# RWKV state of two heads as one block-diagonal 128x128 tile with full products, in a decoder-layer kernel

## The chip, the cores and the metric

The kernel runs on one core of one Trainium2 chip. The metric is the time of one execution on the device in microseconds (us); lower is better. The times of several executions are given as their median with the lowest and the highest. One further execution was taken with the hardware profiler, and all rows shown here come from it.

## The reference

One decoder layer on 2048 tokens of width 1024, in float32. Eight RWKV-7 heads and eight dilated-attention heads of 64 channels each work side by side; then follow an output projection, a layer norm, a mixture of 32 experts with a gated embedding, and a second layer norm. The change concerns the recurrence of the RWKV heads alone:

```python
def step(state, inp):
    r_t, w_t, k_t, v_t, a_t, b_t = inp
    sa = jnp.einsum('bhvk,bhk->bhv', state, a_t)
    state = (state * w_t[:, :, None, :] + sa[..., None] * b_t[:, :, None, :]
             + v_t[..., None] * k_t[:, :, None, :])
    y_t = jnp.einsum('bhvk,bhk->bhv', state, r_t)
    return state, y_t
...
_, y = lax.scan(step, state0, xs)
```

Each head has a state of 64x64, which each token decays, corrects and adds to, and which each token reads.

## The kernel before, in words

`run` (L1945) goes through stages: `project` (input projections and, at its end, `rwkv_prep`, which prepares the RWKV operands and the decays), `mixers` (the recurrence and the attention), `mix_out`, `route`, `ple`, `experts` and `finish`. The change lies in `mixers`.

The recurrence is done in chunks of 128 tokens. Eight heads make four units `u` of two heads, one head in partitions 0 to 63 and the other in 64 to 127 (`H[0]`, `H[1]`). The 2048 tokens make eight column blocks `q` of two chunks `c` each, so there are 4 x 8 x 2 = 64 chunks. A round is a pair of units at one `q`; there are 16 rounds. For each round, `rwkv_front` and `rwkv_inverse` invert the triangular matrices of the chunks, and `rwkv_state` (two streams, `i` = 0 for units 0 and 2, `i` = 1 for units 1 and 3) does the rest. In it:

- L814 to L818 make the masked score matrices: `RB`, and `MJ`, a tile of 2x2x192 elements a partition (head, chunk, 128 score columns and 64 columns of keys). L831 copies the transposed keys into columns 128 to 191 of both (ScalarE); L828 copies the transposed values, `vt`.
- L840 multiplies by `WF`, the inverse's result, and L843 (VectorE, 128x384, once per head) adds the product to all 192 columns of `MJ`.
- L848 makes `pq`; L851 (VectorE) adds the identity to its last 64 columns, giving `E`, 64 columns per chunk with the two heads in the two partition halves, and L854 adds to the rest, giving `Q`.
- Then, for each chunk, in order: L862 (ScalarE) scales the old state by the decay `rho`, giving `st`. L867 and L869 are the new state, for each head the keys of `MJ` times `vt`, plus `E` times `st`, each with 64 columns; L872 (ScalarE) copies it out as `raw`. L877 and L879 are the output, for each head `vt` times the scores of `MJ`, plus `st` times `Q`, 128 columns each, into the head's half of the output partitions; L881 copies it out. L869 and L879 contract over 64 partitions, L867 and L877 over 128; each writes 64 output partitions.

```python
mm(pn[H[h]], MJ[:, h, c, P:192], vt[:, c, H[h]], start=True, stop=first)
if not first:
    mm(pn[H[h]], E[H[h], c], st[H[h]], start=False, stop=True)
...
mm(py[H[h]], vt[:, c, H[h]], MJ[:, h, c, 0:P], start=True, stop=first)
if not first:
    mm(py[H[h]], st[H[h]], Q[H[h], c], start=False, stop=True)
```

The first chunk of all has no old state, and the last computes no new one. Each stream has two PSUM buffers (`self.rps[i]`) for everything it computes, used in turn.

The order of the work: `mixers` hands its streams (two of states, two of inverses, two of fronts, one that combines attention passes, three of attention blocks) to `weave`. A stream yields what its next piece will cost on which engine (`_pe(300)` is 300 ns of TensorE, `_act`, `_dve` and `_pool` give the cost of so many elements), and `weave` lets the stream go on that could start first, attention first while it lags behind a set pace (`late`). The framework's scheduler then puts the instructions of each engine in their final order, with this order as its input; in this stage TensorE's order is not fixed by hand. Other lines of the stage that the text names: L734 (128x128 products with 128 columns, of the inverse), L814 (products of 64 partitions), L717 and L1080 (transposes of 128x128), L1055 and L1058 (attention scores), L1094 (attention output, 64 output partitions per head, the heads one after the other), L1071 (attention's row minimum on VectorE), L665 (GpSimd copies of a front), L676 (a GpSimd memset).

SBUF pools: the recurrence's pools lie on the right side, `rf` among them, and are opened in `rwkv_setup` when the projection's pools close; a tile waits for the tiles that lay in its memory before.

Of the kernel before, what the change touches and what calls it, by code (L numbers as in the profile page):

```python
# [9 lines left out]
F32 = mybir.dt.float32  # L10
F32R = mybir.dt.float32r
I32 = mybir.dt.int32
AF = mybir.ActivationFunctionType
ALU = mybir.AluOpType
# [4 lines left out]
P = 128  # L19
S = 2048  # L20
# [98 lines left out]
def _act(n):  # L119
    return "ACT", 190 + 0.56 * n  # L120


def _dve(n):
    return "DVE", 60 + 1.06 * n
# [6 lines left out]
def _pe(ns):  # L131
    return "PE", ns
# [35 lines left out]
class K:  # L168
# [344 lines left out]
    def rwkv_setup(self, es):  # L513
        tc = self.tc

        pool = lambda name, bufs=1, **k: es.enter_context(tc.tile_pool(name=name, bufs=bufs, reuse_waits="tile", **k))
        self.rl = pool("rl", 2 * ROUNDS, side="right")
        self.rf = pool("rf", side="right")
        self.rv_ = pool("rvt", 2 * ROUNDS, side="right")
        self.rk_ = pool("rk", side="right")  # L520
        self.rps = [pool(f"rps{n}", 2, space=PSUM) for n in range(2)]
        self.state = [None] * 4

        self.small = [self.rf.tile([P, 16, 16], F32, name=name) for name in ("A64", "V64", "tm")]

# [269 lines left out]
    def rwkv_state(self, i, u, q, pp):  # L795

        nc, kp = self.nc, self.rk_
        mm = nc.tensor.matmul
        ps = lambda: self.rps[i].tile([P, BT], F32, name=f"ps{i}", tag=f"ps{i}")
        T = lambda name, shape, bufs=1: kp.tile(shape, F32, name=f"{name}{i}", tag=f"{name}{i}", bufs=bufs)  # L800
        RB = T("RB", [P, 2, 2, 192])
        H = [slice(0, 64), slice(64, 128)]
        col = [slice(c * P, (c + 1) * P) for c in range(2)]
        while "v" not in pp:
            yield None
        rt, v = ([pp[m][:, cs] for cs in col] for m in ("rt", "v"))
        bk = [pp["bk"][:, c] for c in range(2)]
        MJ = T("MJ", [P, 2, 2, 192])
        for h in range(2):
            yield _pe(900)  # L810
            pr = ps().rearrange("p (c k s) -> p c k s", c=2, k=2)
            for c in range(2):
                for m in range(2):
                    mm(pr[:, c, m], bk[c][H[h], m], rt[c][H[h]], start=True, stop=True)  # L814
            yield _dve(2 * P)
            nc.vector.tensor_tensor(out=RB[:, h, :, 0:P], in0=pr[:, :, 0, :], in1=self.c("upi").unsqueeze(1).to_broadcast([P, 2, P]), op=ALU.mult)
            yield _dve(2 * P)
            nc.vector.tensor_tensor(out=MJ[:, h, :, 0:P], in0=pr[:, :, 1, :], in1=self.c("upi").unsqueeze(1).to_broadcast([P, 2, P]), op=ALU.mult)  # L818
        vt = T("vt", [P, 2, P])
        for m in range(2):  # L820
            yield _pe(430 - 215 * m)
            pt = ps().rearrange("p (k s) -> p k s", s=P)
            for j in range(2 - m):
                for c in range(2):
                    nc.tensor.transpose(pt[:, 2 * j + c], v[c] if m else bk[c][:, j], self.c("eye"))
            yield _act((4 - 2 * m) * P)
            if m:
                nc.scalar.copy(vt, pt[:, 0:2])  # L828
            else:
                for j in range(2):  # L830
                    nc.scalar.copy((RB, MJ)[j][:, :, :, P:192], pt[:, 2 * j:2 * j + 2].rearrange("p c (h k) -> p h c k", h=2))  # L831
        while "WF" not in pp:
            yield None
        WF = pp["WF"]
        pm = []
        for h in range(2):
            yield _pe(660)
            pm.append(ps()[:, 0:384].rearrange("p (c s) -> p c s", s=192))
            for c in range(2):
                mm(pm[h][:, c], WF[:, h, c, 64:192], RB[:, h, c], start=True, stop=True)  # L840
        for h in range(2):
            yield _dve(384)
            nc.vector.tensor_tensor(out=MJ[:, h], in0=pm[h], in1=MJ[:, h], op=ALU.add)  # L843
        yield _pe(700)
        pq = ps()[:, 0:384].rearrange("p (c s) -> p c s", s=192)
        for c in range(2):
            for h in range(2):
                mm(pq[H[h], c], WF[:, h, c, 0:64], RB[:, h, c], start=True, stop=True)  # L848
        yield _dve(128)
        E = T("E", [P, 2, 64])  # L850
        nc.vector.tensor_tensor(out=E, in0=pq[:, :, P:192], in1=self.c("eye2").unsqueeze(1).to_broadcast([P, 2, 64]), op=ALU.add)  # L851
        yield _dve(256)
        Q = T("Q", [P, 2, P])
        nc.vector.tensor_tensor(out=Q, in0=pq[:, :, 0:P], in1=pp["rt"].rearrange("p (c s) -> p c s", s=P), op=ALU.add)  # L854
        yt = T("yt", [P, 2 * P])
        for c in range(2):
            first = q == 0 and c == 0
            last = q == 7 and c == 1
            if not first:
                yield _act(64)  # L860
                st = T("st", [P, 64], 2)
                nc.scalar.activation(st, self.state[u], AF.Copy, scale=pp["rho"][:, c:c + 1])  # L862
            if not last:
                yield _pe(300)
                pn = ps()[:, 0:64]
                for h in range(2):
                    mm(pn[H[h]], MJ[:, h, c, P:192], vt[:, c, H[h]], start=True, stop=first)  # L867
                    if not first:
                        mm(pn[H[h]], E[H[h], c], st[H[h]], start=False, stop=True)  # L869
                yield _act(64)  # L870
                raw = T("raw", [P, 64], 4)
                nc.scalar.copy(raw, pn)  # L872
                self.state[u] = raw
            yield _pe(600)
            py = ps()[:, 0:P]
            for h in range(2):
                mm(py[H[h]], vt[:, c, H[h]], MJ[:, h, c, 0:P], start=True, stop=first)  # L877
                if not first:
                    mm(py[H[h]], st[H[h]], Q[H[h], c], start=False, stop=True)  # L879
            yield _act(128)  # L880
            nc.scalar.copy(yt[:, col[c]], py)  # L881
        nc.sync.dma_start(self.y[u * P:(u + 1) * P, q * 2 * P:(q + 1) * 2 * P], yt)
        pp["done"] = True
# [1098 lines left out]
```

## Time and profile before

| | us |
|---|---|
| median of 3 executions (lowest to highest) | 3423.52 (3413.01 to 3430.57) |
| the profiled execution | 3428.44 |
| its span, first to last instruction | 3426.5 |
| busy in the span: TensorE matmuls | 3088.4 |
| TensorE weight loads | 2425.0 |
| VectorE | 2084.3 |
| ScalarE | 1546.0 |
| GpSimd | 666.5 |

PE is TensorE's matmuls, PEld its weight loads, DVE is VectorE, ACT ScalarE, POOL GpSimd, SP the engine that issues most DMAs. A line such as L877 is that line of the kernel. PEclk, the granted clock, is the mean share of 2.4 GHz that TensorE's clock had; it has two levels, 1.2 and 2.4 GHz. Matmuls are pipelined and their ends are modelled: a matmul's duration says less than the distance from its start to the next one's start. An fp32 matmul leaves two records. A few per cent of the matmul records can be missing.

### The profile page before, as it was taken

The numbers are of one execution on the slowest core, as the hardware profiler recorded it, in microseconds if no ns is written. First come the engines' busy times: TensorE is split into PE (matmuls) and PEld (weight loads), VectorE is DVE, ScalarE is ACT, GpSimd is POOL, SyncE is SP. The second block draws the span as 40 slices with busy tenths as digits, with TensorE's granted clock in tenths as the row PEclk, the third lists the DMA queues.
The fourth block names the chain that finished last, engine by engine and source line by source line (L and its number), as shares of the span: only waits on it lengthen the run. The fifth ranks groups of instructions, "written<-read, shape, count | busy, mean of one in ns | idle before, by whom it ended". The sixth has DMA issues, their size and how long they took to land. (4 is left out here: it accounts for less than half of the span.)

```text
span 3426.5 us, 49694 instructions
## 1 busy us (share of the span) xinstructions
PE 3088.4 (90%) x17038; PEld 2425.0 (71%) x17039; DVE 2084.3 (61%) x4542; ACT 1546.0 (45%) x3710; POOL 666.5 (19%) x663
## 2 busy tenths in 40 slices
PE   8989759998899998998999789999999999998880
PEld 6667648776676776777778567778878777786560
DVE  4996324685653643554644768773377778775756
ACT  3443112564444533444434333331177777675642
POOL 0441000353100200200200212222111111111215
PEclk9999879999897977799878799999999999999895
DMA  5213341788525324315310545323289999997745
GB/s 164 80 56 111 81 77 70 218 271 263 114 54 110 86 69 93 84 43 115 101 35 12 143 143 172 112 104 131 80 291 311 321 312 321 308 294 256 277 144 199
DMA packets 364111, 533.21 MB, mean 156 GB/s; under 512 B 92376, under 2 KB 204736, under 8 KB 363840
## 3 DMA queue, kind: packets, MB, share of 16 engines
q1 hardware_dynamic: 333240, 463.94, 43.3%
q0 software_dynamic: 14208, 45.74, 5.7%
q10 hardware_dynamic: 16408, 20.33, 1.8%
q8 instruction: 136, 2.23, 0.3%
q14 instruction: 119, 0.97, 0.1%
HBM read 402.40 MB, written 128.06 MB: 155 GB/s over the span
## 5 line engine op out<-in xcount | busy, mean ns | idle before, releaser
L1697 DVE TENSOR_TENSOR wl<-raw,wh 128x512 fp32r<-128x512 f32 x768 | 477.9, 680 | 89.5 <-ACT wh L1696 89.2
L1696 ACT CAST wh<-raw 128x512 fp32r<-128x512 f32 x768 | 417.3, 620 | 9.8 <-DMA raw<-in_w_up_dram 9.4
L198 PE MATMUL ps<-xh,wh 128*128 128x512 f32 x640 | 263.3, 411 | 0.4 <-ACT xh L322 0.4
L199 PE MATMUL ps<-xl,wh 128*128 128x512 f32 x640 | 259.5, 405 | 1.0 <-DVE xl L323 1.0
L200 PE MATMUL ps<-xh,wl 128*128 128x512 f32 x640 | 258.5, 404 | 0.0
L1074 ACT ACTIVATE pe<-pe,ms 128x256 f32<-128x256 f32 (+1 forms) x384 | 175.3, 458 | 120.1 <-DVE ms L1071 116.0
L1826 POOL DMA_INDIRECT acc<-ysb,ix x48 | 95.8, 1995 | 624.9 <-ACT ysb L1825 401.6
L198 PE MATMUL pe<-wh,XX 128*128 128x512 f32 x480 | 199.2, 415 | 3.8 <-ACT wh L1696 3.8
L199 PE MATMUL pe<-wl,XX 128*128 128x512 f32 x480 | 191.6, 399 | 2.6 <-DVE wl L1697 2.6
L200 PE MATMUL pe<-wh,XX 128*128 128x512 f32 x480 | 190.2, 396 | 0.0
L198 PEld LDWEIGHTS ps<-xh,wh 128*128 128x128 f32 x640 | 125.3, 196 | 34.5 <-issue 2.8
L1071 DVE CUSTOM_DVE_ANT_0 pe<-pl,bias 128x256 f32<-128x256 f32 x216 | 83.5, 420 | 104.3 <-PE pl L1055 75.9
L199 PEld LDWEIGHTS ps<-xl,wh 128*128 128x128 f32 x640 | 125.0, 195 | 30.2 <-DVE xl L323 2.5
L200 PEld LDWEIGHTS ps<-xh,wl 128*128 128x128 f32 x640 | 124.5, 194 | 29.6
L1080 PE MATMUL pl<-eye,pe 128*128 128x128 f32 x600 | 135.1, 318 | 7.7 <-ACT pe L1074 6.1
L1055 PE MATMUL pl<-KK,Q 128*128 128x256 f32 x432 | 118.8, 405 | 16.1 <-DMA KK<-ks 14.9
L1094 PE MATMUL po<-pe,V 128*64 128x128 f32 x1200 | 131.5, 326 | 1.8 <-DVE O L1106 1.3
L198 PE MATMUL pb<-gh,XH 128*128 128x512 f32 x320 | 126.1, 394 | 0.0
L199 PE MATMUL pb<-gl,XH 128*128 128x512 f32 x320 | 125.4, 392 | 0.0
L200 PE MATMUL pb<-gh,XL 128*128 128x512 f32 x320 | 124.9, 390 | 0.0
L1741 PE MATMUL pe<-wh,XX 128*128 128x512 f32 x288 | 119.5, 415 | 5.4 <-ACT wh L1696 5.4
L1742 PE MATMUL pe<-wl,XX 128*128 128x512 f32 x288 | 118.1, 410 | 2.9 <-DVE wl L1697 2.9
(412 smaller groups left out, 7799.8 us busy)
## 6 DMA issues: line engine op xcount, KB each, us to landing
raw<-in_w_gate_dram SPq DMA_DIRECT2D x128, 512.0 KB
raw<-in_w_up_dram SPq DMA_DIRECT2D x128, 512.0 KB
raw<-in_w_down_dram SPq DMA_DIRECT2D x128, 512.0 KB
pk<-pk SPq DMA_DIRECT2D x32, 512.0 KB
pk_t<-pk SPq DMA_DIRECT2D x32, 512.0 KB
KK<-ks SPq DMA_DIRECT2D x64, 256.0 KB
wr<-in_w_in_dram SPq DMA_DIRECT2D x48, 256.0 KB
rkk<-rkk SPq DMA_DIRECT2D x32, 384.0 KB
```

Of the source, the lines that this page charges most:

```text
L198: mm(out, lh, rh, start=first, stop=False)
L199: mm(out, lh, rl, start=False, stop=False)
L200: mm(out, ll, rh, start=False, stop=last)
L1055: mm(pl[:, h], q, toks(KK[:, m, h], n, prev, 2), start=m == 0, stop=m == 1)
L1074: nc.scalar.activation(pe[:, h, w], pe[:, h, w], AF.Exp, bias=m_[h], scale=-1.0, accum_out=s_[h])
L1080: nc.tensor.transpose(pt[:, h, b], pe[:, h, b * P:(b + 1) * P], self.c("eye"))
L1094: mm(o[h * 64:(h + 1) * 64, j], vb[:, h * 64:(h + 1) * 64], tt[:, h, b], start=b == kb[0], stop=b == 1)
L1696: nc.scalar.copy(wh[:, c], raw[:, c])
L1697: nc.vector.tensor_tensor(out=wl[:, c], in0=raw[:, c], in1=wh.bitcast(F32)[:, c], op=ALU.subtract)
L1741: mm(ps, L[:, 0:P], wh, start=first, stop=False)
L1742: mm(ps, L[:, 0:P], wl, start=False, stop=last)
L1826: nc.gpsimd.indirect_dma_start(out=self.acc, out_offset=bass.IndirectOffsetOnAxis(ap=ix[0:r, e, b:b + 1], axis=0), in_=ysb[0:r], in_offset ...
```

## The change

The state of a unit's two heads becomes one 128x128 tile with a head's 64x64 state in each diagonal block, zero elsewhere. Each unit has two such tiles, used in turn; they and two tiles `E`, block-diagonal too, are allocated and cleared once by GpSimd. The new state is one full product of the keys (a tile `MK` of its own) with `vt` plus one of `E` with the state; only the diagonal blocks are copied out, one by ScalarE and one by VectorE, already scaled by the next chunk's `rho`, so the separate scaling is gone. The output takes the two per-head products with the scores as before and one full product of the state with `Q`. The add into `MJ` is split in two, one for the scores and one for the keys, and `E` is written by two instructions. The costs that `rwkv_state` yields to `weave` change with it.

```diff
-        self.state = [None] * 4
+        self.state = [[self.rf.tile([P, P], F32, name=f"S{u}{n}") for n in range(2)] for u in range(4)]
+        self.E = [self.rf.tile([P, 2, P], F32, name=f"E{i}") for i in range(2)]
+        for t in (*(t for ts in self.state for t in ts), *self.E):
+            self.nc.gpsimd.memset(t, 0.0)
...
-        MJ = T("MJ", [P, 2, 2, 192])
+        MJ, MK = T("MJ", [P, 2, 2, P]), T("MK", [P, 2, P])
...
-                for j in range(2):
-                    nc.scalar.copy((RB, MJ)[j][:, :, :, P:192], pt[:, 2 * j:2 * j + 2].rearrange("p c (h k) -> p h c k", h=2))
+                nc.scalar.copy(RB[:, :, :, P:192], pt[:, 0:2].rearrange("p c (h k) -> p h c k", h=2))
+                nc.scalar.copy(MK, pt[:, 2:4])
...
             yield _dve(384)
-            nc.vector.tensor_tensor(out=MJ[:, h], in0=pm[h], in1=MJ[:, h], op=ALU.add)
+            nc.vector.tensor_tensor(out=MJ[:, h], in0=pm[h][:, :, 0:P], in1=MJ[:, h], op=ALU.add)
+            nc.vector.tensor_tensor(out=MK[:, :, H[h]], in0=pm[h][:, :, P:192], in1=MK[:, :, H[h]], op=ALU.add)
...
-        yield _dve(128)
-        E = T("E", [P, 2, 64])
-        nc.vector.tensor_tensor(out=E, in0=pq[:, :, P:192], in1=self.c("eye2").unsqueeze(1).to_broadcast([P, 2, 64]), op=ALU.add)
+        yield _dve(256)
+        E = self.E[i]
+        for h in range(2):
+            nc.vector.tensor_tensor(out=E[H[h], :, H[h]], in0=pq[H[h], :, P:192], in1=self.c("eye2")[H[h]].unsqueeze(1).to_broadcast([64, 2, 64]), op=ALU.add)
...
-            if not first:
+            st, after = (self.state[u][(c + n) % 2] for n in range(2))
+            if not last:
+                yield _pe(224 if first else 448)
+                pn = ps()[:, 0:P]
+
+                mm(pn, MK[:, c], vt[:, c], start=True, stop=first)
+                if not first:
+                    mm(pn, E[:, c], st, start=False, stop=True)
                 yield _act(64)
-                st = T("st", [P, 64], 2)
-                nc.scalar.activation(st, self.state[u], AF.Copy, scale=pp["rho"][:, c:c + 1])
-            if not last:
-                yield _pe(300)
-                pn = ps()[:, 0:64]
-                for h in range(2):
-                    mm(pn[H[h]], MJ[:, h, c, P:192], vt[:, c, H[h]], start=True, stop=first)
-                    if not first:
-                        mm(pn[H[h]], E[H[h], c], st[H[h]], start=False, stop=True)
-                yield _act(64)
-                raw = T("raw", [P, 64], 4)
-                nc.scalar.copy(raw, pn)
-                self.state[u] = raw
-            yield _pe(600)
+                rho = self.rho[:, u, q + c, 1 - c:2 - c]
+                nc.scalar.activation(after[H[0], H[0]], pn[H[0], H[0]], AF.Copy, scale=rho[H[0]])
+                yield _dve(64)
+                nc.vector.tensor_scalar_mul(after[H[1], H[1]], pn[H[1], H[1]], rho[H[1]])
+            yield _pe(640)
             py = ps()[:, 0:P]
             for h in range(2):
-                mm(py[H[h]], vt[:, c, H[h]], MJ[:, h, c, 0:P], start=True, stop=first)
-                if not first:
-                    mm(py[H[h]], st[H[h]], Q[H[h], c], start=False, stop=True)
+                mm(py[H[h]], vt[:, c, H[h]], MJ[:, h, c], start=True, stop=first)
+            if not first:
+                mm(py, st, Q[:, c], start=False, stop=True)
```

## Rows read from the trace of the kernel before

**Rows 1.** The page: span, and each engine's busy time.

```profile
span 3426.5 us, 49694 instructions
...
PE 3088.4 (90%) x17038; PEld 2425.0 (71%) x17039; DVE 2084.3 (61%) x4542; ACT 1546.0 (45%) x3710; POOL 666.5 (19%) x663
```

**Rows 2.** Busy times by stage: length, PE, PEld, DVE, ACT, POOL; PEclk, DMA share, GB/s.

```profile
860.00:1930.00 1070.00, 1019.44 (x7262) 785.85 (x7261) 541.44 (x1938) 460.66 (x1572) 138.61 (x226) 0.83 0.33 79
```

**Rows 3.** Groups by line, PE, 860 to 1930: busy us, mean ns | idle before.

```profile
L877 PE MATMUL ps<-MJ,vt 128*64 128x128 f32 x240 | 59.1, 342 | 0.7 <-DVE AW L713 0.7
...
L869 PE MATMUL ps<-st,E 64*64 64x64 f32 x216 | 39.4, 270 | 0.0
```

**Rows 4.** Who waited for whom, PE, 860 to 1930: us, times, longest.

```profile
PE ps L848 <- DVE MJ L843: 11.4, 2, 10.2
```

**Rows 5.** Timeline of PE, high clock, recurrence: start us, us, instruction, count.

```profile
1155.44 0.32 PE L869 MATMUL ps<-st,E 64*64 64x64 f32 x2
1155.70 0.33 PE L867 MATMUL ps<-vt,MJ 128*64 128x64 f32 x2
...
1156.21 0.43 PE L877 MATMUL ps<-MJ,vt 128*64 128x128 f32 x2
1156.57 0.43 PE L879 MATMUL ps<-Q,st 64*64 64x128 f32 x2
```

**Rows 6.** Timeline of PE, high clock, other shapes.

```profile
1167.87 0.44 PE L1094 MATMUL po<-pe,V 128*64 128x128 f32 x4
1168.24 1.16 PE L734 MATMUL ps<-U,AB 128*128 128x128 f32 x8
1169.33 1.16 PE L642 MATMUL ps<-pk_t 64*128 64x128 f32 x8
...
1171.58 0.38 PE L1080 MATMUL pl<-eye,pe 128*128 128x128 f32 x2
1171.80 0.28 PE L740 MATMUL ps<-t,X 128*128 128x128 f32 x1
...
1253.39 0.44 PE L1080 MATMUL pl<-eye,pe 128*128 128x128 f32 x2
1253.76 0.44 PE L1094 MATMUL po<-pe,V 128*64 128x128 f32 x4
```

**Rows 7.** Timeline of PE, low clock, recurrence.

```profile
1289.91 0.69 PE L877 MATMUL ps<-MJ,vt 128*64 128x128 f32 x2
1290.53 0.69 PE L879 MATMUL ps<-Q,st 64*64 64x128 f32 x2
```

**Rows 8.** Timeline of PE, low clock, 128x128 with 128 columns.

```profile
1295.00 1.11 PE L1080 MATMUL pl<-eye,pe 128*128 128x128 f32 x4
1295.91 0.63 PE L717 MATMUL ps<-eye,pk_t 128*128 128x128 f32 x2
```

**Rows 9.** Groups by line, ACT and DVE, 860 to 1930.

```profile
L862 ACT ACTIVATE st<-raw,rho 128x64 f32<-128x64 f32 x58 | 19.9, 348 | 0.5
...
L872 ACT COPY raw<-ps 128x64 f32<-128x64 f32 x58 | 12.3, 212 | 76.0 <-PE ps L869 74.2 <-PE ps L867 1.7
...
L843 DVE TENSOR_TENSOR MJ<-ps,MJ 128x384 f32<-128x384 f32 x60 | 32.9, 551 | 6.5 <-PE ps L840 5.5
L854 DVE TENSOR_TENSOR Q<-ps,pk_t 128x256 f32<-128x256 f32 x30 | 12.4, 413 | 0.0
L851 DVE TENSOR_TENSOR E<-ps,ct 128x128 f32<-128x128 f32 x30 | 8.7, 289 | 7.7 <-PE ps L848 6.9
```

**Rows 10.** POOL: a group by line, 800 to 1960, and the timeline's row.

```profile
L676 POOL MEMSET V<- 64x256 f32 x16 | 4.9, 306 | 327.2 <-DMA inv<-V 256.0 <-DVE AW L713 39.5 <-DVE ms L1071 31.5
...
843.61 2.59 POOL L665 COPY C<-AB 32x128 f32<-32x128 f32 x8 [13.73 <-DVE AB L660]
```

**Rows 11.** Busy times of two stretches of the stage (columns as in Rows 2).

```profile
1200.00:1400.00 200.00, 187.93 (x1150) 141.63 (x1149) 80.48 (x288) 70.90 (x239) 19.21 (x35) 0.69 0.34 77
...
1900.00:1980.00 80.00, 60.93 (x383) 45.18 (x383) 55.25 (x98) 27.73 (x69) 19.85 (x14) 0.72 0.52 142
```

More of the change, by code (lines that the diff above doesn't have):

```diff
@@ L817, in rwkv_state @@
             yield _dve(2 * P)
-            nc.vector.tensor_tensor(out=MJ[:, h, :, 0:P], in0=pr[:, :, 1, :], in1=self.c("upi").unsqueeze(1).to_broadcast([P, 2, P]), op=ALU.mult)
+            nc.vector.tensor_tensor(out=MJ[:, h], in0=pr[:, :, 1, :], in1=self.c("upi").unsqueeze(1).to_broadcast([P, 2, P]), op=ALU.mult)
         vt = T("vt", [P, 2, P])
```

## The prediction

> **What bounds the kernel now.** The page comes first: the span is 3426.5 us and TensorE is busy for 90% of it [rows 1]; the reader should see an engine that hardly rests anywhere. Then the busy times by stage: the changed code runs only in the stage from 860 to 1930 us, where TensorE is busy for 1019 of 1070 us, VectorE for 541, ScalarE for 461 and GpSimd for 139, at a granted clock of 0.83 [rows 2]. A clock of 0.83 between the levels 1.2 and 2.4 GHz means that about 2 x (1 - 0.83) = 34% of this stage ran at the lower one. The groups by line show that the recurrence is a large customer: L877 has 240 recorded matmuls and 59 us of modelled busy time, L869 has 216 and 39 us, and L867 and L879 are alike [rows 3] (an fp32 matmul is two records). Last the waits: TensorE's largest total in this stage is 11.4 us, 10.2 of it in one piece [rows 4]; nearly all the rest of the 51 us outside its busy time is pieces of that kind. So what counts in this stage is the time from one matmul's start to the next one's, and that is read from the timeline.
>
> **The matmuls, one chunk at a time.** There are 64 chunks (4 units x 8 column blocks x 2); 60 compute a new state, 56 of these with the E product, and 60 outputs use the old state. At the high clock the four products of a new state start 0.26 us apart (1155.44, 1155.70) and the four of an output 0.36 us apart (1156.21, 1156.57) [rows 5]: 1.04 + 1.44 = 2.48 us a chunk. The head's halves lie in different parts of the array, yet one does not start before the other's turn is over.
>
> After, a new state is two 128x128 products of 128 columns. L734 has that shape: four of them take 1.09 us (1168.24 to 1169.33), so two take 0.55 [rows 6]. An output is L877 for both heads back to back, then one full product. L1094 has the first shape, two heads on 64 columns each: one pair in 0.37 us (1167.87 to 1168.24) [rows 6]. A lone 128x128 product costs 0.37 behind another shape (1253.39 to 1253.76) and 0.22 among its own (1171.58 to 1171.80) [rows 6]; I take 0.37, since a 64-column product precedes it. So the output is 0.74 us. Saved at the high clock: 56 x 0.49 + 60 x 0.70 = 69 us, and about 2 on the eight products of first chunks (two half products become one full, and the pair goes back to back): 71.
>
> At the low clock the output's products start 0.62 us apart (1289.91, 1290.53) [rows 7], 1.72 times as far, so the state's four come to 0.26 x 1.72 x 4 = 1.79 and the output's to 2.48. Four passes of 128x128 take 0.91 us there (1295.00 to 1295.91) [rows 8], 1.67 times the 0.55. After: 0.91 and 0.74 x 1.67 = 1.24. Saved: 56 x 0.88 + 60 x 1.24 = 124 us. A third of the time at about 0.57 of the speed holds some 22% of the work: 0.78 x 71 + 0.22 x 124 = **83 us** of TensorE's time.
>
> Bounds: if the two new-state products always stand alone they cost 2 x 0.37, if always among their own shape 2 x 0.22; if the scheduler separates the heads' L877, the output costs 3 x 0.36 = 1.08, at best 0.37 + 0.22 = 0.59. That is 56 x 0.30 + 60 x 0.36 = 38 us to 56 x 0.60 + 60 x 0.85 = 85 at the high clock, 45 to 99 in the mixture.
>
> **A rule that speaks against it.** The starts in [rows 5] never overlap between heads. The Trainium skill, TensorEngine Tiling (Array Packing), Overview and Key Properties, says that products with small dimensions should be put on independent tiles of the array, which run side by side, up to two-fold for one halved dimension. By that rule the two heads' products already cost one between them, four products two, and the full ones, half of them zeros, would save nothing: 3424 us. This trace agrees with it for L1094, where two heads follow each other directly, and not for the alternating lines of the state; the sum goes by the rows.
>
> **Everything else.** ScalarE loses L862 (348 ns) and the L872 copy (212 ns), 60 each at most [rows 9], and gets one scaled copy of 64x64 per new state, for which I take L862's 348: 12 us less. The chain from the end of the E product to the next use is one evacuation on two engines instead of two on ScalarE, 0.2 us shorter a chunk. VectorE gets the other half: 64x64 from PSUM, between nothing beyond a small fixed time and L851's 289 ns; I take 0.25 us, 15 us in all. L843 (551) splits into a 128x256 and a 128x128 add, nearest L854 (413) and L851 (289) [rows 9]: 151 ns more, 64 times, 10 us. E on 64 rows twice costs the second time as much again, since the elements per row stay: 32 x 289 ns = 9 us. Together 34 us on an engine with 529 us free in the stage; the cover is TensorE's own work. On the path it delays the next products by 0.3 us (the adds, which hold PSUM buffers that L848 waits for) and 0.3 us (E) per unit; with no cover 32 x 0.6 = 19 us. The new half evacuations queue behind attention's VectorE work, and a product with the state now waits for both engines. No semaphore waits for anything later than before: the next chunk's rho is computed in the projection stage.
>
> GpSimd gets ten memsets, eight of 128 and two of 256 elements a row; L676 (256) takes 306 ns, so 2.0 (by length) to 3.1 us [rows 10]. GpSimd waits 13.73 us before its first copy at 843.61 [rows 10], which hides them; if the memory they clear is released only when that copy is due, it and the first front slip by those 3 us. No DMA is added, and SP's queue keeps its order.
>
> **Given back.** The last unit of each of the four heads' pairs (8 of 64 chunks) runs in 1900 to 1980, where TensorE is busy for only 61 of 80 us [rows 11]: 10 of the 83 us don't count there. The start costs 1 to 3. As TensorE has 8% less to do, waits that DMAs and VectorE end become longer: I add a fifth to the 51 us, 10; bounds 0 and, with VectorE's 19 uncovered too, 45. Sum: -83 + 10 + 3 + 10 = **-60 us**. The profiled execution took 3428.4 us, 4.9 above the median shown (3423.5): 3368 by its own time, 3363 beside the median.
>
> **The rivals.**
> 1. *The clock comes back too.* The short products don't fill the array; denser work could shorten the low stretches. Each us at the low clock loses about 0.43. If a third of the 364 us goes, 120 x 0.43 = 52 more: 3311. For it: some stretches of the stage run at full clock; against: low stretches also follow waits that the change doesn't touch.
> 2. *Mostly eaten by waits.* Separated products (45), 10 lost at the end, and 30 more of waits and VectorE on the path: 3415 to 3424, no change. For it: the scheduler mixes streams freely, and the order of the whole stage is planned anew since the planner's costs change. Against: every other engine is half idle [rows 2]. The tiling rule would give the same time; on [rows 5] I leave it 0.02.
> 3. *Slower, by the clock.* Fewer TensorE columns against unchanged waits could hold the stage low: 1200 to 1400 had 0.69 [rows 11]. At that value all through, 62% of some 1080 us instead of 364 us is low: 300 x 0.43 = 130 us lost against 60 gained, 3493. It decides where the stage's clock falls under about 0.75 (180 us more at the low level eat 77, the gain and half a per cent). Against: the removed products are themselves sparse.
>
> **How the numbers follow.** Half a per cent, 17 us, is about what a measurement here can tell. Forecast (3325 to 3395) 0.60; the clock too 0.15; eaten by waits 0.18, a quarter of it still faster by over 0.5%; slower 0.07. So faster 0.79, same 0.14, slower 0.07. The range takes in the first rival's time and reaches the near end of no change: 3305 to 3421, leaving out some 0.15 to 0.2.
>
> **What the profile would show.** Right: half as many records for the new state and three quarters for the output; state matmuls of one chunk in 1.2 to 1.5 us instead of 2.5; the stage 50 to 80 us shorter, all later stages equal in length; VectorE up by some 34 us, ScalarE down by 12. Wrong: the full products 0.4 us or more apart, the stage's clock under 0.78, or TensorE's time outside its busy time in the stage over 90 us.

## The result, and the profile after

The changed kernel takes 3294.45 us (median of 4 runs, 3288.43 to 3298.42) against 3418.27 us of the kernel before, timed beside it (4 runs, 3412.90 to 3430.57): a ratio of 0.9615 [0.9575, 0.9656]. The forecast was faster, by 60 us; the gain is 124. The time lies 11 us below the range, and nearest to the first rival, "the clock comes back too", at 3311.

The page of the profiled execution after (3298.42 us) answers to [rows 1]: span, busy times, and the granted clock in 40 slices.

```profile
span 3296.5 us, 49200 instructions
...
PE 2947.2 (89%) x16686; PEld 2350.5 (71%) x16687; DVE 2111.6 (64%) x4698; ACT 1532.7 (46%) x3650; POOL 674.0 (20%) x673
...
PEclk9999888999889998898997899999999999999895
```

TensorE's busy time fell by 141 us, more than the span (130). VectorE rose by 27 us and ScalarE fell by 13, where 34 and 12 were forecast. To see where the time went, the execution is cut at the same events in both kernels: 860 us, the last recurrence product, the start of the routing products, the end. First the kernel before (columns as in [rows 2]):

```profile
0.00:860.00 860.00, 740.29 (x3397) 581.66 (x3399) 520.70 (x881) 318.23 (x663) 202.29 (x219) 0.93 0.48 139
860.00:1979.00 1119.00, 1055.91 (x7537) 814.01 (x7537) 574.43 (x1994) 479.24 (x1620) 149.61 (x235) 0.83 0.33 81
1979.00:2277.00 298.00, 274.26 (x1508) 224.14 (x1507) 224.78 (x386) 107.47 (x234) 73.44 (x49) 0.97 0.42 142
2277.00:3426.00 1149.00, 1017.94 (x4600) 805.15 (x4598) 764.36 (x1283) 641.02 (x1194) 241.18 (x160) 0.94 0.73 244
```

And the same stretches after:

```profile
0.00:860.00 860.00, 741.88 (x3393) 583.18 (x3395) 521.82 (x879) 318.02 (x661) 202.23 (x220) 0.93 0.48 140
860.00:1859.00 999.00, 927.95 (x7247) 749.57 (x7246) 610.47 (x2162) 467.25 (x1567) 159.37 (x247) 0.90 0.37 91
1859.00:2150.00 291.00, 262.97 (x1453) 214.67 (x1453) 215.29 (x376) 105.69 (x229) 71.09 (x47) 0.95 0.42 144
2150.00:3296.00 1146.00, 1014.39 (x4598) 803.11 (x4596) 764.06 (x1283) 641.77 (x1194) 241.36 (x160) 0.94 0.74 245
```

The stage with the recurrence gives 120 of the 130 us, the two after it 10. In it two things changed together: TensorE has 128 us less to be busy with, and the granted clock went from 0.83 to 0.90. By 2 x (1 - clock) x length that is 380 us at the lower level before and 200 after. TensorE's time outside its busy time went from 63 to 71 us.

The timeline of one chunk after, at the high clock (start us, duration us, engine, instruction, records), answers to [rows 5, 6]:

```profile
1128.23 0.49 PE L870 MATMUL ps<-vt,MK 128*128 128x128 f32 x2
...
1128.56 0.39 PE L872 MATMUL ps<-S,E 128*128 128x128 f32 x2
...
1128.78 0.38 PE L1084 MATMUL pl<-eye,pe 128*128 128x128 f32 x2
...
1129.01 0.30 ACT L875 ACTIVATE S<-ps,rho 64x64 f32<-64x64 f32 x1
...
1129.09 0.44 PE L881 MATMUL ps<-MJ,vt 128*64 128x128 f32 x4
...
1129.34 0.29 DVE L877 TENSOR_SCALAR S<-ps,rho 64x64 f32<-64x64 f32 x1
...
1129.46 0.49 PE L883 MATMUL ps<-Q,S 128*128 128x128 f32 x2
...
1129.79 0.27 PE L1084 MATMUL pl<-eye,pe 128*128 128x128 f32 x1
```

The new state takes 0.33 + 0.22 = 0.55 us, the output pair 0.37 and the full output product 0.33: here the prices taken, 0.55 and 0.74, are met or beaten. The two halves of the evacuation, one on ScalarE and one on VectorE, do not run side by side: VectorE starts 0.03 us after ScalarE ends.

The groups by line after (records, busy us, mean ns, idle before) answer to [rows 3, 9]:

```profile
L883 PE MATMUL ps<-Q,S 128*128 128x128 f32 x120 | 29.8, 331 | 0.0
L881 PE MATMUL ps<-MJ,vt 128*64 128x128 f32 x256 | 28.8, 299 | 0.9 <-DVE S L877 0.6 <-DVE tm L687 0.3
L870 PE MATMUL ps<-vt,MK 128*128 128x128 f32 x120 | 25.8, 300 | 0.1
L872 PE MATMUL ps<-S,E 128*128 128x128 f32 x112 | 22.7, 286 | 7.5 <-DVE E L857 7.5
...
L875 ACT ACTIVATE S<-ps,rho 64x64 f32<-64x64 f32 x60 | 18.5, 308 | 29.3 <-PE ps L872 26.7 <-PE ps L870 2.1
...
L847 DVE TENSOR_TENSOR MJ<-ps,MJ 128x256 f32<-128x256 f32 x64 | 26.9, 420 | 32.6 <-PE ps L844 32.1
L857 DVE TENSOR_TENSOR E<-ps,ct 64x128 f32<-64x128 f32 x64 | 18.4, 287 | 6.9 <-PE ps L853 5.9
L848 DVE TENSOR_TENSOR MK<-ps,MK 128x128 f32<-128x128 f32 x64 | 17.9, 279 | 0.0
L877 DVE TENSOR_SCALAR S<-ps,rho 64x64 f32<-64x64 f32 x60 | 17.4, 291 | 17.9 <-ACT S L875 16.5
```

The record counts are as forecast: half as many for the new state (232 against 464 of the two lines before), three quarters for the output. The waits of TensorE in the stage after (us in total, times, longest) answer to [rows 4]: single pieces again, the largest near the end of the stage, and almost none with the new evacuation.

```profile
PE pa L1315 <- DMA y<-y: 18.6, 1, 18.6
PE ps L872 <- DVE E L857: 7.5, 1, 7.5
```

### The profile page after: what moved, and what is told of

Its sections match the earlier page's. It is cut to its first block, busy times and chain, and to the rows that moved or that the text cites. A ratio compares the mean times of both kernels' runs of the same rounds, so it can differ in the third digit from the quotient of the medians.

```text
span 3296.5 us, 49200 instructions
## 1 busy us (share of the span) xinstructions
PE 2947.2 (89%) x16686; PEld 2350.5 (71%) x16687; DVE 2111.6 (64%) x4698; ACT 1532.7 (46%) x3650; POOL 674.0 (20%) x673
## 5 line engine op out<-in xcount | busy, mean ns | idle before, releaser
L1084 PE MATMUL pl<-eye,pe 128*128 128x128 f32 x600 | 124.1, 299 | 3.7 <-ACT pe L1078 3.2
L198 PE MATMUL pa<-woh,YH 128*128 128x512 f32 x256 | 111.3, 435 | 11.7 <-DVE h L1349 6.8
```

Of the source, the lines that this page charges most:

```text
L198: mm(out, lh, rh, start=first, stop=False)
L1084: nc.tensor.transpose(pt[:, h, b], pe[:, h, b * P:(b + 1) * P], self.c("eye"))
```

## The experiments

Eighteen kernels ran, each beside the kernel before on the same chip. The kernel before was timed beside all of them, 49 executions, 3395 to 3449 us, median 3425. Two columns of the table are worked out from an execution's time and its mean granted clock, and averaged over the executions of a kernel: the low time, 2 x (1 - clock) x time, that is the time at the lower of the two levels; and the time at full clock, time - 0.42 x low time. The 0.42 is 1 - 1/1.72, by the distances at the two levels in [rows 5, 7]; among the 49 executions of the kernel before the time itself rises by 0.38 us with each us of low time. "Alternating" marks kernels in which TensorE changes from a head's 128-partition half product to its 64-partition one and back, as in the kernel before; "full" those with the change's full products in both places.

| run | products | median us | ratio to before | low time | at full clock |
|---|---|---|---|---|---|
| before | alternating | 3425 | 1 | 650 | 3151 |
| e2_new_plan | alternating | 3403.9 | 0.9931 [0.9896, 0.9965] | 583 | 3162 |
| e12_before_order_a | alternating | 3403.7 | 0.9947 [0.9906, 0.9989] | 564 | 3161 |
| e13_before_order_b | alternating | 3370.2 | 0.9873 [0.9821, 0.9925] | 521 | 3153 |
| e11_all_but_full | alternating | 3361.1 | 0.9836 [0.9804, 0.9868] | 509 | 3148 |
| e18_all_but_full_b | alternating | 3370.6 | 0.9853 [0.9804, 0.9903] | 491 | 3167 |
| e4_full_state_only | full state | 3335.2 | 0.9719 [0.9658, 0.9780] | 475 | 3134 |
| e5_full_output_only | full output | 3343.4 | 0.9741 [0.9684, 0.9797] | 518 | 3125 |
| e3_heads_adjacent | half, side by side | 3324.6 | 0.9672 [0.9598, 0.9746] | 505 | 3108 |
| after | full | 3294.5 | 0.9615 [0.9575, 0.9656] | 458 | 3102 |
| e1_old_plan | full | 3311.7 | 0.9671 [0.9612, 0.9730] | 482 | 3107 |
| e14_after_order_a | full | 3321.5 | 0.9719 [0.9675, 0.9763] | 520 | 3104 |
| e15_after_order_b | full | 3291.8 | 0.9645 [0.9605, 0.9686] | 458 | 3100 |
| e16_two_evacuations | full | 3297.2 | 0.9628 [0.9584, 0.9673] | 476 | 3096 |
| e17_two_evacuations_b | full | 3288.3 | 0.9598 [0.9554, 0.9642] | 452 | 3099 |
| e8_rows_adjacent | full | 3308.4 | 0.9655 [0.9608, 0.9703] | 500 | 3099 |
| e6_dense_padding | full, 4 more | 3344.2 | 0.9766 [0.9723, 0.9809] | 443 | 3156 |
| e7_sparse_padding | full, 4 half more | 3357.1 | 0.9809 [0.9764, 0.9854] | 467 | 3163 |
| e9_sparse_long | full, 8 half more | 3441.2 | 1.0063 [1.0035, 1.0092] | 464 | 3246 |
| e10_dense_long | full, 11 more | 3452.4 | 1.0095 [1.0069, 1.0121] | 447 | 3263 |

The row of e12 leaves out the three longest of its ten executions (3423 to 3439 us, more than 1.5% above its shortest). With all ten its median is 3412 us and its low time 588; its time at full clock stays 3161.

### The planner's costs alone: e1 and e2

The change also alters what `rwkv_state` yields to `weave`, and so the order of the stage. e1 is the changed kernel with the old costs, e2 the kernel before with the new ones.

```diff
 # e1, against after
-        yield _dve(256)
+        yield _dve(128)
...
-                yield _pe(224 if first else 448)
+                if not first:
+                    yield _act(64)
+                yield _pe(300)
...
-                yield _dve(64)
...
-            yield _pe(640)
+            yield _pe(600)
```

e2 is this edit the other way round in the kernel before.

> The changed kernel, but its recurrence yields the planner's costs of the kernel before, so that only the order in which the stage's work is woven differs. Theory (the dense products themselves lift TensorE's granted clock): 3280 to 3315 us, time at the low clock from 860 us to the end of the recurrence 180 to 240 us as in the changed kernel (about 200). Rival (the new order, not the products, removed the low stretches): 3340 us or more, with 300 us or more at the low clock.

> The kernel before, with the planner's costs of the changed kernel and its own products. Theory (dense products): within 25 us of the kernel before (3418), low clock in the stage 310 to 400 us. Rival (order): 3370 us or less, low clock 250 us or less.

e1 took 3311.7 us and e2 3403.9. The new costs alone give some 0.7% and do not explain the 3.9%. But both move the low time with hardly a change at full clock: e2 has 67 us less of it than the kernel before although its instructions are the same. The order of the stage reaches the clock.

### The products apart: e3, e4 and e5

e3 is the kernel before with one edit: both heads' first products, then both heads' second ones. Nothing becomes a full product, and no evacuation, memset or cost changes.

```diff
 # e3, against before
-                    if not first:
+                if not first:
+                    for h in range(2):
                         mm(pn[H[h]], E[H[h], c], st[H[h]], start=False, stop=True)
...
-                if not first:
+            if not first:
+                for h in range(2):
                     mm(py[H[h]], st[H[h]], Q[H[h], c], start=False, stop=True)
 # e4, against after: the output's second product in halves again
-            if not first:
-                mm(py, st, Q[:, c], start=False, stop=True)
+                if not first:
+                    mm(py[H[h]], st[H[h], H[h]], Q[H[h], c], start=False, stop=True)
 # e5, against after: the new state in halves again
-                mm(pn, MK[:, c], vt[:, c], start=True, stop=first)
-                if not first:
-                    mm(pn, E[:, c], st, start=False, stop=True)
+                for h in range(2):
+                    mm(pn[H[h], H[h]], MK[:, c, H[h]], vt[:, c, H[h]], start=True, stop=first)
+                    if not first:
+                        mm(pn[H[h], H[h]], E[H[h], c, H[h]], st[H[h], H[h]], start=False, stop=True)
```

> The kernel before, with the per-head products regrouped: both heads' first products, then both heads' second ones, so that two heads follow each other directly on different parts of the array. If halves that follow each other run side by side (as the attention output's do), four 64-column products of a state take about 0.6 us and four of an output about 0.75 us instead of 0.99 and 1.40, and the time falls by 50 us or more, to 3370 or less, without any full product. If the gain needs full 128x128 products (a 64x64 product still waits for the change of the array's tiling and leaves the clock low), the time stays above 3395.

> The changed kernel with the output per head as before (four products that alternate) and the new state by full products. By the products' measured distances at the high clock, the new state gives 0.99 - 0.62 = 0.37 us a chunk and the output 1.40 - 0.85 = 0.55 us, so about two fifths of the gain should be here if it adds up: 3418 - 50 = 3368 (3350 to 3390). If the clock is lifted only when no sparse cluster is left, the gain is under 25 us: 3395 or more.

> The changed kernel with the new state per head, alternating as before, and the output with both heads' first products adjacent and one full product. If the parts add up by TensorE's time alone, 0.55 us of the 0.92 us a chunk is saved: ratio to the kernel before 0.980 to 0.985. If one cluster of alternating half products is enough to hold the clock low, low time from 860 us to the recurrence's end stays over 300 us. If the low time is lost with either half of the change (the new state alone gave 199 us and ratio 0.972), it is 190 to 260 us here too and the ratio 0.965 to 0.975, and the two parts don't add up.

e3 is the surprise: 3324.6 us, 0.9672 [0.9598, 0.9746], and at full clock 3108 against the changed kernel's 3102, with no full product at all. TensorE's timeline of e3 in one chunk, at the high clock, shows why:

```profile
1145.67 0.34 PE L867 MATMUL ps<-vt,MJ 128*64 128x64 f32 x4
1145.94 0.33 PE L1082 MATMUL pl<-eye,pe 128*128 128x128 f32 x1
...
1147.94 0.33 PE L870 MATMUL ps<-st,E 64*64 64x64 f32 x4
1148.20 0.44 PE L878 MATMUL ps<-MJ,vt 128*64 128x128 f32 x4
1148.57 0.44 PE L881 MATMUL ps<-Q,st 64*64 64x128 f32 x4
1148.94 0.44 PE L825 MATMUL ps<-eye,v_t 128*128 128x128 f32 x2
```

Four records, the products of both heads, are over in the 0.27, 0.26 and 0.37 us that one head's product took in [rows 5]. The four products of an output now take 0.74 us, the price of the changed kernel's output, and the four of a new state 0.53. Summed over the stage from one record's start to the next one's, TensorE's idle time left out and low-clock distances divided by 1.72, the four lines of the state cost 143.1 us before, 77.6 after and 78.8 in e3.

So two half products on different column halves do run side by side when they follow each other directly; the kernel before changed shape between them and lost it. The Trainium skill, TensorEngine Tiling (Array Packing), Key Properties, says both: that different tiles can execute in parallel, and that changing the tiling mode, not just the tile, drains the engine. e3 agrees, with 0.26 us for two heads where alternating shapes took 0.26 for each.

e4 and e5 price the two places: against the mean of the five alternating reorderings and the kernel before, 3157 us at full clock, the full state saves 23 us and the full output 32, together 55. Both at once save 56 (the mean of the six kernels marked full up to e17 is 3101). The parts add up.

### Do sparse products hold the clock low: e6, e7, e9 and e10

The theory at this point was that of the first rival: alternating half products leave the array poorly filled, and the clock comes back when they go. These four add products that are overwritten by the ones behind them, so that each output stays the same: e6 four full ones a chunk, e7 four alternating half ones, e10 eleven full ones, e9 the eight alternating half ones of the kernel before.

```diff
 # e6, against after (e10: range(11))
             py = ps()[:, 0:P]
+            for n in range(4):
+                mm(py, MK[:, c], vt[:, c], start=True, stop=True)
 # e9, against after (e7: its first loop alone)
+            for n in range(2):
+                mm(py[H[n], 0:64], MK[:, c, H[n]], vt[:, c, H[n]], start=True, stop=True)
+                mm(py[H[n], 0:64], E[H[n], c, H[n]], vt[H[n], c, H[n]], start=True, stop=True)
+            for n in range(2):
+                mm(py[H[n]], vt[:, c, H[n]], MJ[:, n, c], start=True, stop=True)
+                mm(py[H[n]], vt[H[n], c, H[n]], Q[H[n], c], start=True, stop=True)
```

> The changed kernel with four more full 128x128x128 products per chunk into the output's bank ahead of the output (overwritten, no result changes): about 8 x 0.112 = 0.9 us a chunk, 57 us of TensorE's time, which gives back what the change saves at the high clock. Theory (density lifts the clock): low time stays at 170 to 230 us, time up by 45 to 65 us on the changed kernel, ratio to the kernel before 0.975 to 0.982. Rival (the clock came with less queueing on TensorE, so any work of that length brings the low stretches back): low time over 320 us, ratio 0.99 or more.

> The changed kernel with four alternating half products of 64 columns per chunk ahead of the output (128x64, 64x64, 128x64, 64x64, as the new state had before; overwritten): about 1.0 us a chunk at the high clock, 62 us, nearly the length of the dense padding. Theory (sparse alternating products pull the clock down): low time over 290 us, and at least 30 us slower than the dense padding; ratio 0.99 to 1.0. Rival (density doesn't matter): same low time and same time as the dense padding, within 15 us.

> The changed kernel with eight alternating half products per chunk ahead of the output, the shapes and the order of the kernel before (four of 64 columns, four of 128; overwritten): 2.4 us a chunk at the high clock, 154 us. The short sparse padding (1.0 us a chunk) did not bring the low stretches back. If a long run of sparse products holds the clock low (before, eight of them stood in a row; none of the other kernels has more than four), the low time from 860 us to the recurrence's end goes over 320 us and the time over the dense padding of the same length by 50 us or more: ratio to the kernel before over 1.02. If density does not matter to the clock here, low time under 230 us and the same time as the long dense padding within 20 us: ratio 1.00 to 1.01.

> The changed kernel with eleven more full 128x128x128 products per chunk ahead of the output (overwritten): 22 x 0.112 = 2.5 us a chunk, 158 us at the high clock, the length of the long sparse padding. Density theory: low time 100 to 190 us and a ratio to the kernel before of 0.995 to 1.01. If low stretches come with the length of the stage rather than with density, low time over 230 us and ratio over 1.015.

The stage of e9 by windows, from 860 us to the last recurrence product, columns as in [rows 2]:

```profile
860.00:1979.00 1119.00, 1068.16 (x8237) 827.79 (x8235) 616.81 (x2153) 469.21 (x1562) 152.85 (x245) 0.94 0.34 81
```

And that of e10:

```profile
860.00:1965.00 1105.00, 1051.63 (x8559) 883.77 (x8560) 584.07 (x2128) 458.41 (x1544) 150.31 (x240) 0.94 0.33 80
```

e9 carries eight alternating half products in every chunk, beside the change's own, in a stage exactly as long as that of the kernel before, and its clock is 0.94, not 0.83. Sparse or dense makes no more than 24 us of low time (443 and 467, 447 and 464). The theory falls: sparse products added to the changed kernel bring back no low stretches. The same runs confirm the prices: 64 chunks of four or eleven full products at 0.22 us would be 56 and 155 us, and at full clock e6 and e10 stand 54 and 161 us above the changed kernel; eight alternating ones at 2.48 us a chunk [rows 5] would be 159, and e9 stands 144 above it.

### All of the change but the full products: e11 and e18

e11 keeps the tiles, the memsets, the evacuation and the costs of the change, and brings back the alternating half products in both places: the edits of e4 and e5 together. e18 is e11 with 600 for 640 in the last cost.

> The changed kernel (block-diagonal tiles, evacuation on two engines with the scale, split adds, the new costs) with the eight alternating half products of the kernel before in place of the full ones. If the products' shape and order are the cause of the whole gain, both in TensorE's time and in the clock: ratio 0.985 to 1.005, low time 300 to 400 us. If the removed scaling, the split evacuation or the order of the stage is what lifts the clock: ratio 0.975 or less, low time under 250 us.

> All of the change but the full products, in a second order (planner's cost of the output's products 600). The first order had a low time of 509 us and a ratio of 0.984. If the products bring the clock part: low time 540 us or more here, ratio 0.99 or more. If the evacuation does: 450 to 520 us, ratio 0.975 to 0.985.

At full clock e11 and e18 (3148 and 3167) are back among the alternating kernels. With the rest of the change kept, nothing remains of its gain there. But their low time (509 and 491) stays far below the 650 of the kernel before, and with it their ratios, 0.9836 and 0.9853. By the expectation of e18 that speaks for the evacuation; e16 and e17 below test it. In the profile's window of the stage of e11 the clock is that of the changed kernel, with alternating products in it:

```profile
860.00:1907.00 1047.00, 1006.46 (x7588) 781.54 (x7588) 607.30 (x2154) 470.24 (x1565) 155.61 (x244) 0.90 0.36 86
```

### The order alone: e12 to e15

That left the order. Four kernels change one cost and nothing else: e12 the kernel before with 340 for 300 in the new state's cost, e13 with 560 for 600 in the output's; e14 the changed kernel with 244 and 488 for 224 and 448, e15 with 600 for 640.

```diff
 # e13, against before
-            yield _pe(600)
+            yield _pe(560)
```

> The kernel before with the planner's cost of the new state's products at 340 instead of 300; the same instructions in another order. If the order alone makes the clock part (the kernel before is a bad draw): ratio 0.98 to 0.995, low time 250 to 340 us, as with the other reordering (0.993). If the low time belongs to what the kernel before does (its products or its two evacuations one behind the other): ratio 0.996 to 1.004, low time 350 to 420 us.

> The kernel before with the planner's cost of the output's products at 560 instead of 600. As for the first reordering: order alone, ratio 0.98 to 0.995; what the kernel does, 0.996 to 1.004.

> The changed kernel with the planner's cost of the new state's products at 244 and 488 instead of 224 and 448. If the change itself lifts the clock: ratio 0.957 to 0.968, low time 170 to 240 us. If its own order was a good draw: ratio 0.97 or more, low time over 260 us.

> The changed kernel with the planner's cost of the output's products at 600 instead of 640. As for the first: change itself, ratio 0.957 to 0.968; a good draw, 0.97 or more.

e13 computes what the kernel before computes, with the same instructions, and takes 3370.2 us, 0.9873 [0.9821, 0.9925]: 1.3% for a number that a planner reads. e14 loses 27 us of the changed kernel's gain in the same way. At full clock none of the four leaves its group by more than 4 us; the low time moves, from 521 to 650 among the orders of the kernel before, and from 458 to 520 for these two of the changed kernel.

### Rows side by side, and the evacuation: e8, e16 and e17

e8 tries on the scores' products what e3 does for columns: the two heads lie in different row halves, and their products are made to follow each other directly, into different PSUM buffers. e16 takes the new evacuation off PSUM: ScalarE copies the whole 128x128 tile, then both engines scale from the copy. e17 is e16 with 600 for 640.

```diff
 # e8, against after: the last of its three places
+        prs = [ps().rearrange("p (c k s) -> p c k s", c=2, k=2) for _ in range(2)]
+        for c in range(2):
+            for m in range(2):
+                for h in range(2):
+                    mm(prs[h][:, c, m], bk[c][H[h], m], rt[c][H[h]], start=True, stop=True)
 # e16, against after
-                nc.scalar.activation(after[H[0], H[0]], pn[H[0], H[0]], AF.Copy, scale=rho[H[0]])
+                raw = T("raw", [P, P], 2)
+                nc.scalar.copy(raw, pn)
+                yield _act(64)
+                nc.scalar.activation(after[H[0], H[0]], raw[H[0], H[0]], AF.Copy, scale=rho[H[0]])
...
-                nc.vector.tensor_scalar_mul(after[H[1], H[1]], pn[H[1], H[1]], rho[H[1]])
+                nc.vector.tensor_scalar_mul(after[H[1], H[1]], raw[H[1], H[1]], rho[H[1]])
```

> The changed kernel with the three groups of 64-row score products (of the front, the inverse and the recurrence, some 155 us of TensorE's time in all) regrouped so that the two heads, which lie in the upper and the lower 64 rows, follow each other directly, into two PSUM buffers. If row halves run side by side as column halves do, a pair of products takes about 0.25 us instead of 0.45 and the time falls by 40 us or more on the changed kernel, ratio to the kernel before 0.95 or less. If row halves don't overlap, the ratio stays at 0.96 to 0.97.

> The changed kernel, but the new state is first copied out by ScalarE (128x128) and then scaled into the two diagonal blocks by ScalarE and VectorE, so that two evacuations stand behind each other as in the kernel before, 0.27 us more a chunk on the chain. If the shorter chain brings the clock part: low time of the whole execution 550 us or more (the changed kernel and its reorderings have 458 to 520), ratio 0.978 or more. If it comes with the products or the order: 450 to 520 us, ratio 0.96 to 0.972.

> The same with the planner's cost of the output's products at 600 instead of 640, another order. Same expectations: the chain, 550 us or more and ratio 0.978 or more; the products or the order, 450 to 520 us and 0.96 to 0.972.

e8 brings nothing, 3099 us at full clock. But its trace shows that the edit seldom reached TensorE: in most of the stage the scheduler still runs one head's eight records by themselves, as in the first two lines here. In three of the 32 groups of this line the records of both heads do alternate from the first to the last, as in the other two:

```profile
1342.03 1.16 PE L826 MATMUL ps<-pk_t 64*128 64x128 f32 x8
1343.11 0.33 PE L1094 MATMUL pl<-eye,pe 128*128 128x128 f32 x1
...
1197.91 1.17 PE L826 MATMUL ps<-pk_t 64*128 64x128 f32 x16
1199.01 0.49 PE L880 MATMUL ps<-vt,MK 128*128 128x128 f32 x2
```

One head's eight records take 1.08 us, and the sixteen of both heads 1.10: side by side, two heads cost the time of one here too. The Trainium skill, TensorEngine Tiling (Array Packing), Tiling Modes, Available Configurations, lists two tiles of 64 rows by 128 columns; the trace agrees in these three groups. Over the stage the records of this product stand 129 ns apart at full clock, against 131 after, with such groups so few. So e8 does not answer its question: what that order would be worth over the whole stage stays open, and so does why the scheduler separates the heads.

e16 and e17 lengthen the chain of each state by one evacuation and end level with the changed kernel (its runs 3288 to 3298; theirs have medians of 3297.2 and 3288.3). The evacuation chain does not bound the stage. No run is faster than the changed kernel beyond what its interval allows.

## Why the prediction was wrong

**The products.** This step held. From start to start, TensorE's idle time left out, the state's lines take 171.9 us of the stage before and 80.0 after: 92 us of TensorE's time against the 83 forecast. At full clock the saving is 143.1 - 77.6 = 65 us, not 71, within its bounds of 38 and 85. The products after cost what was taken: the new state 0.56 us a chunk (0.55), the output 0.73 (0.74), with the full output product 0.37 us from its successor on average (two records of 184 ns). Those before were a little cheaper than the rows chosen, 0.97 and 1.41 us for 1.04 and 1.44. And 69 of the 171.9 us before lay in low stretches, 69 / 1.72 = 40 of 143.1 us of work or 28%, where the mixture assumed 22; after, only 6 of the 80.0 us did.

**The rule that speaks against it.** The prediction set it aside on [rows 5], because alternating lines never overlapped, and that is what e3 corrects. The rows priced the kernel before nearly rightly. They did not show that the halves can't overlap, only that they don't in that order. The full products are worth what they are because they put an end to the alternation; adjacency does so as well. "The full products would save nothing" is true against e3, and not against the kernel before.

**The step that failed: the clock.** "0.78 x 71 + 0.22 x 124" keeps the low share of the stage as it was. The low time of an execution fell from 650 to 458 us, and 192 x 0.42 = 80 us is most of the gain; the remaining 49 us (3151 - 3102) are the products, less what was given back. In the stage some 180 us of low time went, and only 69 - 6 = 63 of them lay under the state's own lines: the sum had no term for the other work of the stage. The first rival had this term, with a third of 364 us; about half went. Its reason found no support: in e9 added sparse products did not lower the clock. The third rival, a stage clock under 0.75, did not come.

**Where the clock came from.** The means of the two groups (before, e2, e11, e12, e13 and e18; after, e1 and e14 to e17) are 3157 and 3101 us at full clock, and do not overlap (3148 to 3167 and 3096 to 3107): 56 us for the products, in any order. Their low times are 553 and 474 us on average, and do overlap: 79 x 0.42 = 33 us that go with the groups. The closest pairs, e11 against after and e18 against e15, show 51 and 33 us of low time, that is 21 and 14 us. The rest is the draw of one order: the kernel before has 97 us more low time than its group's mean, 41 us of time, the changed kernel 16 us less, 7 us. 56 + 33 + 41 + 7 = 137; the kernel before, 6 us quicker at full clock than its group, and the changed kernel, 1 slower, make it 130, the difference of the medians in the table. By the means of the ratios, 0.9907 and 0.9646, the change is worth 2.6%, some 90 us; the rest of its 3.9% is that the kernel before has the worst order of all that were run.

What in an order makes low stretches longer stays open. In the two profiled executions their number in the stage is about the same, 19 and 20, and their mean length 20 and 10 us. Falls of the clock often come behind waits: in the 5 us ahead of a fall TensorE was idle for 26% of the time before and 30% after, ahead of a rise for 3% in both, over the stage for 6 and 7%. But ahead of 8 of the 19 falls before it was not idle for more than 0.01 us. No run isolates a cause, nor what of the 33 us comes from the products and what from the rest of the change.

**The small terms.** "Given back", 23 us: the waits rose by 8 (forecast 10). At full clock the products save 65 us, the group means differ by 56 and the two kernels by 49: 9 to 16 us were given back. The scatter of some 10 to 20 us within a group does not tell the tail and the start apart. The memsets:

```profile
847.41 0.79 POOL L526 MEMSET S<- 128x128 f32 x5 [20.07 <-DMA ks<-ol]
...
849.43 0.60 POOL L669 COPY C<-AB 32x128 f32<-32x128 f32 x2
```

In GpSimd's timeline after, the first front's copy starts at 849.43 us, not at 843.61 [rows 10], because the memory to be cleared is released only at 847.41: the slip the prediction named, 6 us and not 3. VectorE's instructions came out as priced: 420 + 279 - 551 = 148 ns more for the split add (151), 287 ns for the second half of `E` (289), 291 for its half evacuation (250). The shorter evacuation was wrong: ScalarE's 0.30 and VectorE's 0.29 us follow each other, so the chain is 0.6 us where it was 212 + 348 ns; e16 and e17, with a longer chain still, show that it does not matter. "All later stages equal" missed 10 us.

## What to carry to other kernels

Where half products of two heads alternate between shapes, first put those of equal shape side by side: e3 gets the same TensorE time as the block-diagonal tiles with two moved loops. Price products by the distance from start to start in the order in which they stand, and ask what another order of the same products would give before a rule is put aside. Read in the trace whether the new order is the one that ran: e8's was there in 3 of 32 groups. And before a change of the granted clock is credited to an edit, run both kernels under two or three other orders; here one number read by a planner moved the time by 1.3%, so a forecast for such a stage needs some 30 us on either side for the order alone.

## What the runs showed of the hardware that was not expected

- Two half products on different column halves that follow each other directly take the time of one: 0.26 us (64 columns) and 0.37 us (128 columns), where alternating shapes took 0.26 and 0.36 for each. Two on different row halves do the same where their records alternate: 1.10 us for the sixteen of two heads, 1.08 for the eight of one (e8).
- Two engines that write disjoint diagonal blocks of one tile took turns: VectorE's half waited for ScalarE's in 16.5 of its 17.9 us of idle time. The program asks for it: in the trace VectorE's instruction waits for the semaphore that ScalarE's raises. Whether the chip alone would let them run side by side was not tried.
- The low time of a kernel differs from one execution to the next: the kernel before ran from 3395 to 3449 us in 49 executions, 1.6% apart, with the same instructions.
